# Joint stage of an encoder layer: stores on other queues, seven pairs begun, and the second sequence's key, value and query ahead of the first's merge

## The chip, the cores and the metric

One core of a Trainium2 chip. The metric is the device time of the whole kernel in microseconds, the median of several executions.

## What is computed

One layer of an encoder in fp32, for two independent sequences of 512 tokens and width 1024 ("prompt" is sequence 0, "sample" is sequence 1). Cut to what matters here:

```python
x = x + 0.5 * swiglu(rms_norm(x, ffn1_norm), ...)            # first FFN, D_FF = 2816
h = rms_norm(x, mix_norm)
aq, ak, av, mq, mk, mv, gate_pre, o_pre, g_att, g_mlstm = split(h @ w_in)
aq = apply_rope(rms_norm(aq per head, q_norm), cos, sin)     # 8 heads of 64
ak = apply_rope(rms_norm(ak per head, k_norm), cos, sin)     # 2 key/value heads
att = gqa_block_attention(aq, ak, av)                        # softmax over all 512 keys
mem = mlstm_bidirectional(mq, mk, mv, gate_pre, ..., o_pre)  # 4 heads of 128, forward and backward
merged = sigmoid(g_att) * (att @ w_up_att) + sigmoid(g_mlstm) * (mem @ w_up_mlstm)
x = x + merged @ w_out
x = x + 0.5 * swiglu(rms_norm(x, ffn2_norm), ...)            # second FFN
return rms_norm(x, final_norm)
```

## The kernel before, in words

**Tiles.** A sequence lies transposed, as 8 tiles of 128 channels x 512 tokens. An fp32 product is made of fp32r products of high and low halves (`hi`, `lo`), three for each pair of tiles; a weight is split into its halves by one operation of ScalarE and one of VectorE, from a raw tile (four buffers, `wr`) into a split tile (four buffers, `w8`). Weights that the second sequence needs again are stored split to DRAM (`wpark`, L236) and loaded from there (L228). Work tiles of 128x512 come from a ring of eleven (`T2`) and one of four (`F2`). PSUM has the banks `mm` (3), `pss` (2), `pst` (2) and `pso` (1).

**Stages.** The first FFN for both sequences (to about 660 us); then mixing (to about 1477 us); then the second FFN. Mixing is written as a generator `mix(s, ...)` for each sequence, `m0` and `m1`, which the main program resumes by `next` so that stages of the two alternate.

**The end of the first FFN.** The down products give each output tile in turn, first of sequence 0, then of sequence 1; `done1` stores each and adds up squares. At the last tile of sequence 0 it makes the statistics and all eight normed tiles in one go (`normed`, store to `xnbuf`, `put`); the statistics of sequence 1 come behind the key/value product of mix (`early`).

**Mixing of sequence 0.** `tok_proj` for key/value/gates, then for query (L724). The raw query and key rows go to DRAM (`qkbuf`). Then the joint stage, `Joint`: eleven pairs of output columns (4 of mLSTM query and key, 2 of output gates, 4 of memory gates, 1 of attention gates) are computed for both sequences together with a Strassen-like scheme of seven block products for each pair. `begin` makes the first two of them (24 products of 128x512), which need only the left normed blocks of sequence 0; `right_sums` makes the sums of blocks (`xc`, L253, L257 to L260) that the other five need (60 products); `whole` makes those, and all 84 for a pair not begun. Five pairs are begun (`BEGUN`). The results (`emit`) go to DRAM: `joint_q`, `joint_k` as halves (L1429, L1430), the others through a tanh (L1433, L1436). Behind each `whole` stands one of eleven *pieces* of sequence 0: gates, key piece, four query pieces, four maxima pieces, scales. A query piece loads a raw row, sums squares (L778, L779), takes the reciprocal root on GpSimd (L165, L167, tile `rs`), applies rope on VectorE, splits, transposes on PE in two groups of four (L956) into the one bank `pso`, copies (L957) and stores (`qtbuf`, L958). The pieces share four rows.

**Behind it.** Attention of sequence 0 loads `kv` and `qT` from these buffers; then four memory heads (scores L1163, transposes L1205, products L1213, statistics L177 and L187, with the units of `merge_att` between), then `merge_mem` (L740, tiles `pss` and `pst`), which needs the memory heads' output `mem`. Then `m1` runs its own key/value and query products, keeping rows in SBUF, and `q_rope` and `k_turn` lie beside eight output units of sequence 0 (`out_unit`). Attention, memory heads, merge and output units of sequence 1 follow.

**What sets the order.** The code's order and small shifts of priority (`shifted`) are turned into one instruction list for each engine before the run; an engine takes its list in order. SyncE (SP) issues nearly all transfers before the change, and its queue is in order as well: a store that waits for its data holds up the loads behind it.

## Time and profile before

| | us |
|---|---|
| median of 3 runs (lowest, highest) | 2130.81 (2128.25, 2133.09) |
| the profiled execution: time | 2128.62 |
| the profiled execution: span in the trace | 2126.7 |
| PE busy | 2053.2 |
| mean granted clock of PE | 0.988 |

The span runs from the first instruction to the last. A row of the timeline gives start, duration, engine, line, operation, tiles, shape and count; in brackets the idle time before it and what ended that. A row of waits gives the line that waited, what released it, then total us, times and longest. `L307` is the line of the Strassen-like products in both FFNs and in the joint stage, so its rows are told apart by their time.

### The profile page before, as it was taken

The page shows a single profiled execution, that of the slowest core. Times are in us where ns is not written, and L with a number is a line of the kernel's source. Part 1 is how long each engine was busy: PE and PEld are TensorE (multiplying, and loading weights), DVE is VectorE, ACT ScalarE, POOL GpSimd, SP SyncE. Part 2 cuts the span into 40 slices and gives each one's busy share as a digit, 9 for nine tenths or more (in the row PEclk, how much of TensorE's full clock was granted, in tenths as well). Part 3 has the DMA queues.
Part 4 walks back from the last instruction along what each step waited for, and adds up shares of the span by engine and source line. Part 5 has one row for each costly group of instructions (what it writes and reads, how often), then busy time and mean ns, then how long its engine had stood idle before and what let it go on. Part 6 is the DMA issues. An engine that isn't in the chain of part 4 may idle for free.

```text
span 2126.7 us, 27181 instructions
## 1 busy us (share of the span) xinstructions
PE 2053.2 (97%) x9356; PEld 1675.9 (79%) x9356; DVE 1547.5 (73%) x2611; ACT 973.5 (46%) x1801; POOL 140.2 (7%) x156
## 2 busy tenths in 40 slices
PE   8999999999998899899998999989999999999998
PEld 6888888888887677687877877778888888888887
DVE  6887776767785686649686778674878777786696
ACT  7544444532224444346674446542644444443222
POOL 1000000001013002200012110001000000000000
PEclk9999999999999999999999999999999999999999
DMA  9655654799756955556567862667755564499753
GB/s 285 196 191 165 225 177 158 240 340 335 260 194 251 285 173 159 148 188 234 208 208 260 279 214 86 217 200 258 247 168 193 177 219 169 159 342 349 271 199 114
DMA packets 322506, 464.82 MB, mean 219 GB/s; under 512 B 21600, under 2 KB 180336, under 8 KB 320960
## 3 DMA queue, kind: packets, MB, share of 16 engines
q1 hardware_dynamic: 321776, 461.82, 64.3%
q0 software_dynamic: 592, 1.27, 0.3%
q8 instruction: 74, 1.21, 0.2%
q14 instruction: 64, 0.52, 0.1%
HBM read 295.07 MB, written 167.94 MB: 218 GB/s over the span
## 4 chain that ended last, share of the span: by engine, by line
PE 86%; DVE 5%; DMA 4%; ACT 2%; issue 1%; POOL 1%; SPq 0%; DVEq 0%; POOLq 0%; ACTq 0%
PE pss L307 20%; PE pst L307 13%; PE mm L307 11%; PE mm L574 8%; PE mm L740 8%; PE pss L574 4%; PE pst L574 4%; PE mm L724 4%; PE pso L574 3%; PE pso L1069 1%; PE pss L1042 1%; PE pst L1061 1%; PE pso L724 1%; PE pst L740 1%; PE pso L1213 1%
## 5 line engine op out<-in xcount | busy, mean ns | idle before, releaser
L307 PE MATMUL pss<-xc,w 128*128 128x512 f32 x1320 | 325.3, 395 | 8.3 <-ACT w L265 6.7
L307 PE MATMUL pst<-xc,w 128*128 128x512 f32 x1320 | 324.0, 390 | 2.3 <-ACT xc L252 2.3
L307 PE MATMUL mm<-xc,w 128*128 128x512 f32 x1320 | 315.4, 391 | 4.5 <-ACT f L315 1.7
L307 PEld LDWEIGHTS pss<-xc,w 128*128 128x128 f32 x1320 | 248.3, 190 | 65.2 <-ACT w L265 7.1
L307 PEld LDWEIGHTS mm<-xc,w 128*128 128x128 f32 x1320 | 247.1, 188 | 59.4 <-ACT f L315 3.9
L307 PEld LDWEIGHTS pst<-xc,w 128*128 128x128 f32 x1320 | 247.7, 188 | 54.3 <-ACT xc L252 3.0
L265 ACT ACTIVATE w<-t 128x512 fp32r<-128x512 f32 x220 | 134.4, 628 | 204.9 <-DVE t L291 56.3
L266 DVE TENSOR_TENSOR w<-t,w 128x512 fp32r<-128x512 f32 x220 | 149.8, 696 | 84.6 <-ACT w L265 81.0
L574 PE MATMUL mm<-rt,w 128*128 128x512 f32 (+1 forms) x819 | 191.0, 387 | 3.8 <-DVE xs L591 3.8
L574 PEld LDWEIGHTS mm<-rt,w 128*128 128x128 f32 x819 | 152.6, 189 | 34.2 <-DVE xs L591 4.2
L307 PE MATMUL pss<-xc,f 128*128 128x512 f32 x660 | 162.2, 395 | 6.3 <-DVE t L1479 6.2
L307 PEld LDWEIGHTS pss<-xc,f 128*128 128x128 f32 x660 | 125.4, 191 | 34.4 <-DVE t L1479 8.0
L642 ACT ACTIVATE w<-t 128x512 fp32r<-128x512 f32 x82 | 51.6, 632 | 111.5 <-PE pst L574 68.3
L642 ACT ACTIVATE w<-wr 128x512 fp32r<-128x512 f32 x72 | 44.6, 630 | 125.7 <-PE pso L574 68.6
L266 DVE TENSOR_TENSOR w<-wr,w 128x1024 fp32r<-128x1024 f32 x55 | 67.3, 1223 | 38.8 <-ACT w L265 38.7
L574 PE MATMUL pss<-rt,w 128*128 128x512 f32 x396 | 93.7, 389 | 0.0
L574 PE MATMUL pst<-rt,w 128*128 128x512 f32 x396 | 93.7, 389 | 0.0
L574 PEld LDWEIGHTS pss<-rt,w 128*128 128x128 f32 x396 | 74.3, 188 | 15.4
L574 PEld LDWEIGHTS pst<-rt,w 128*128 128x128 f32 x396 | 74.3, 188 | 15.4
L265 ACT ACTIVATE w<-wr 128x1024 fp32r<-128x1024 f32 x55 | 58.2, 1058 | 51.6 <-PE pst L307 17.9
L740 PE MATMUL mm<-mh,w 128*128 128x512 f32 x256 | 79.9, 391 | 0.0
L643 DVE TENSOR_TENSOR t<-pst,t 128x512 fp32r<-128x512 f32 x96 | 65.0, 687 | 19.7 <-ACT t L642 18.5
(405 smaller groups left out, 3549.7 us busy)
## 6 DMA issues: line engine op xcount, KB each, us to landing
rt<-rbuf SPq DMA_DIRECT2D x154, 512.0 KB, 5.7
wr<-in_ffn_w_gate_dram SPq DMA_DIRECT2D x62, 512.0 KB, 5.3
wpark<-w SPq DMA_DIRECT2D x60, 512.0 KB, 4.1
w<-wpark SPq DMA_DIRECT2D x60, 512.0 KB, 5.4
rbuf<-tab SPq DMA_DIRECT2D x102, 256.0 KB, 3.9
wr<-in_ffn_w_up_dram SPq DMA_DIRECT2D x44, 512.0 KB, 4.2
wr<-in_w_in_dram SPq DMA_DIRECT2D x40, 512.0 KB, 4.9
rbuf<-f SPq DMA_DIRECT2D x72, 256.0 KB, 4.1
```

The costliest lines, as they stand in the source:

```text
L265: pin(nc.scalar.activation(t[:, 0], src, AF.Copy))
L266: pin(V_.tensor_tensor(t[:, 1], src, f(t[:, 0]), op=ALU.subtract))
L307: nc.tensor.matmul(p, a[:, k, :], xt[:, b, k, :], start=(first and k == 0 and i == 0), stop=(k == HK_ - 1 and i == 2), skip_group_check=True)
L574: nc.tensor.matmul(p, u[:, a, d * P:(d + 1) * P], r[:, b, ts], start=(first and q == 0 and k == 0), stop=(q == len(us) - 1 and k == 2), sk ...
L642: nc.scalar.activation(hi, src, AF.Copy)
L643: (eng or V_).tensor_tensor(lo, src, f(hi), op=ALU.subtract)
L724: nc.tensor.matmul(p[b][:, :N], src(k)[a][:, bs], w_[:, kl, :], start=(k == 0 and i == 0), stop=(k == KD - 1 and i == 2))
L740: nc.tensor.matmul(p, a[:, k, :], b, start=(k == 0 and i == 0), stop=(k == n - 1 and i == 2))
L1042: nc.tensor.matmul(p, qT[:, h, b * P:(b + 1) * P], kv[:, hk * 2 + j, :], start=(j == 0), stop=(j == 1))
L1061: nc.tensor.transpose(p[:, b * P:(b + 1) * P], Ps[b][:, kb * P:(kb + 1) * P], ident)
L1069: nc.tensor.matmul(po, Vst[:, kv_, hk, :], w, start=(kv_ == 0 and i == 0), stop=(kv_ == 3 and i == 1))
L1213: nc.tensor.matmul(po, vm[:, a, t, hs_], b, start=(t == 0 and n == 0), stop=(t == 3 and n == 2))
```

## The change

1. **End of the first FFN.** `done1` makes the normed tiles of sequence 0 one by one, each with a tile of sequence 1 (in the order of d + 4), and the statistics of sequence 1 at its fourth tile; `early` is gone. The `xnbuf` store goes to GpSimd's queue.
2. **Stores.** `wpark` and the low halves of joint q and k, the output gates and the value rows go to GpSimd's queue; high halves, memory and attention gates, `kept`, `qkbuf`, `qtbuf` and the key rows go to ScalarE's. The loads of a piece (`qkbuf`, `ebuf`) go to GpSimd's queue. `kvbuf`, `qtbuf` and `qkbuf` exist once for each sequence.
3. **Seven pairs begun** in place of five, in the order (1, 2), (3, 4), (5), (6) behind the four steps of right sums.
4. **Sequence 1 goes the way of sequence 0**: its key/value and query rows go to DRAM, and its eleven pieces replace `k_turn` and `q_rope`. Its two products stand behind the last memory head of sequence 0 and ahead of that sequence's `merge_mem`; the pieces stand one behind each `merge_mem` unit, with rows of the common ring and the bank `pso`. Five of sequence 0's output units follow at once, three go into the queue of sequence 1's attention.
5. **Dealing.** The six attention gates that a sequence computes itself go to DRAM and come back at `merge_att`; the `merge_att` units are dealt evenly over the memory heads, in the order 6, 7, 0 to 5; `merge_mem` alternates between `pss` and `mm`; the maxima of sequence 1 leave its attention for its pieces.

The diff, cut to its core:

```diff
-            nc.sync.dma_start(d[:, i], f(t))
+            nc.gpsimd.dma_start(d[:, i], f(t))          # wpark
...
         def q_piece(b, rows, bank):
             t, o, m, out = rows
-            nc.sync.dma_start(t, qkbuf[:, b, :])
+            nc.gpsimd.dma_start(t, qkbuf[s][:, b, :])
...
                 nc.scalar.activation(out, p, AF.Copy)
-                nc.sync.dma_start(qtbuf[:, g * 4:g * 4 + 4, b * P:(b + 1) * P], out.rearrange("p (h t) -> p h t", t=P))
+                nc.scalar.dma_start(qtbuf[s][:, g * 4:g * 4 + 4, b * P:(b + 1) * P], out.rearrange("p (h t) -> p h t", t=P))
...
+        queue.extend(merge_att(d) for d in (6, 7, 0, 1, 2, 3, 4, 5))
         for h in range(HM):
...
-            queue.append(merge_att(2 * h))
-            fill(1)
+            fill(-(-len(queue) // (8 - 2 * h)))
             mem_out(h, Ts)
-            queue.append(merge_att(2 * h + 1))
-            fill(99)
-
+            fill(-(-len(queue) // (7 - 2 * h)))
+            if h in (1, 2) and not s:
+                for d in range(4):
+                    prep1(4 * (h - 1) + d)
+        flush()
+
+        pieces = yield
         mh, ml = A([P, KD, S], F32R, "mh"), A([P, KD, S], F32R, "ml")
         for d in range(KD):
             mem_gate(d)
             go(merge_mem(d))
+            if pieces:
+                pieces.pop(0)([T2() for _ in range(4)], PO)
         flush()
-        yield None
-
+        for q in pieces:
+            q([T2() for _ in range(4)], PO)
...
     def done1(s, d, _):
         nc.sync.dma_start(xbuf[s][:, d, :], xs[s][:, d, :])
-        accs[s] = sq_add(xs[s][:, d, :], accs[s], "R", eng=V_ if s == 0 and d == KD - 1 else None)
-        if s == 0 and d == KD - 1:
-            mid_stats(0)
-            for i in (B11, B21):
-                xm[i] = xc_tile()
-            for k in range(KD):
+        last = d == (KD - 1, HK_ - 1)[s]
+        accs[s] = sq_add(xs[s][:, d, :], accs[s], "R", eng=V_ if last else None)
+        if last:
+            mid_stats(s)
+        if s:
+            k = (d + HK_) % KD
+            if k % HK_ == 0:
+                xm[(B11, B21)[k // HK_]] = xc_tile()
+            with shifted(20):
                 xt = xs[0][:, k, :]
                 normed(xt, gm, R[0], k)
-                nc.sync.dma_start(xnbuf[:, k, :], xt)
+                nc.gpsimd.dma_start(xnbuf[:, k, :], xt)
                 put(xm[B11 if k < HK_ else B21], k % HK_, xt)
...
-                nc.sync.dma_start(to[:, 0, :], hi)
-                nc.sync.dma_start(to[:, 1, :], lo)
+                nc.scalar.dma_start(to[:, 0, :], hi)
+                nc.gpsimd.dma_start(to[:, 1, :], lo)
...
-    BEGUN = 5
+    BEGUN = 7
...
-        if k + 1 < BEGUN:
-            jn.begin(k + 1, jn.left(k + 1))
+        for j in ((1, 2), (3, 4), (5,), (6,))[k]:
+            jn.begin(j, jn.left(j))
...
-    next(m0)
-    m1 = mix(1, lambda k: [t[:, k, :] for t in nhl[1]], None, lambda: stats2(0), prep2)
-    next(m1)
-    next(m0)
-    next(m1)
-    acc2[0] = next(m0)
-    next(m1)
-    next(m1)
-    acc2[1] = next(m1)
+    m0.send([])
+    m1 = mix(1, lambda k: [t[:, k, :] for t in nhl[1]], lambda: stats2(0), prep2)
+    pieces = next(m1)
+    units, acc = m0.send(pieces)
+    go(*units[:5])
+    flush()
+    acc2[0] = acc
+    m1.send(units[5:])
+    units, acc = m1.send([])
+    go(*units)
+    flush()
```

The order of the instructions at three places. First SP, at the start of the joint stage, where the rows of the right sums are first loaded (from `xbuf` and `xnbuf`; `wr` are raw weights of pairs). Before:

```order
L206 DMA wr_5743<-in_w_in_dram 128x8x128
L1445 DMA kept_0_289<-f_395_5522 128x512
L206 DMA wr_5799<-in_w_in_dram 128x8x128
L1429 DMA joint_q_5524<-t_390_5517 128x512
L1541 DMA t_389_5516<-xbuf_111 128x512
L1430 DMA joint_q_5524<-t_391_5518 128x512
L1541 DMA t_387_5514<-xnbuf 128x512
```

and now:

```order
L206 DMA wr_5642<-in_w_in_dram 128x8x128
L206 DMA wr_5678<-in_w_in_dram 128x8x128
L206 DMA wr_5734<-in_w_in_dram 128x8x128
L206 DMA wr_5770<-in_w_in_dram 128x8x128
L206 DMA wr_5825<-in_w_in_dram 128x8x128
L1480 DMA t_385_5571<-xbuf_111 128x512
L1480 DMA t_383_5569<-xnbuf 128x512
```

The stores have left SP, and two more raw weights, those of the two further pairs, stand ahead of the first row.

Second PE, behind the products of the last memory head of sequence 0 (its statistics are L177 and L187 in both). Before, `merge_mem` of sequence 0 (operand `mem`) follows:

```order
L1213 MATMUL pso_8999<-t_968_9039,Vm_8451 128x512
L177 MATMUL pst_9051<-ident,t_969_9048 128x128 x4
L187 MATMUL pst_9061<-ident,rs_9058 128x128
L740 MATMUL pst_9144<-mem_8209,w_9089 128x512 x9
L187 MATMUL pst_9061<-ident,rs_9058 128x128 x3
```

and now products of key and value of sequence 1 (`xh`, `xl` are its normed tiles as halves):

```order
L1147 MATMUL pso_9076<-t_944_9116,Vm_8482 128x512
L724 MATMUL mm_9191<-w_9188,xh_8762 128x272
L724 MATMUL mm_9191<-w_9188,xl_8763 128x272
L724 MATMUL mm_9191<-w_9188,xh_8762 128x272 x2
L724 MATMUL mm_9191<-w_9188,xl_8763 128x272
L724 MATMUL mm_9191<-w_9219,xh_8762 128x272
L177 MATMUL pst_9128<-ident,t_945_9125 128x128 x4
```

The products of 128x272 now stand around the statistics; `merge_mem` has gone behind all of them and the query's.

Third GpSimd (POOL) beside `merge_mem` of sequence 0, where the pieces of sequence 1 now stand: it issues the stores of split weights (L236), loads the key row (L889) and the first query row (L912), makes low halves of the merged rows (L643) and the reciprocal roots:

```order
L236 DMA wpark_9694<-w_9691 128x1024 x2
L236 DMA wpark_9808<-w_9805 128x1024
L889 DMA t_1001_9519<-qkbuf_5201 128x512
L236 DMA wpark_9808<-w_9805 128x1024
L236 DMA wpark_9936<-w_9933 128x1024
L643 TENSOR_TENSOR ml_9441<-mg_8233,mh_9440 128x512
L236 DMA wpark_9936<-w_9933 128x1024
L165 TENSOR_SCALAR rs_9527<-ssk_9524 128x8
L167 TENSOR_TENSOR rs_9527<-rs_9527,nhalf 128x8
L643 TENSOR_TENSOR ml_9441<-mg_8233,mh_9440 128x512
L912 DMA t_1016_9600<-qkbuf_5201 128x512
```

Before, this stretch of POOL's list held the six L643 operations and nothing else ahead of sequence 1's gates; now a load of a row can be issued only when the stores listed ahead of it have their split weights.

177 lines of the change are left out of this document (57 added, 120 removed).

## The prediction

> **What bounds the kernel now.** I read the page first: who is busy, and who stands in the chain that ended last.
>
> ```profile
> PE 2053.2 (97%) x9356; PEld 1675.9 (79%) x9356; DVE 1547.5 (73%) x2611; ACT 973.5 (46%) x1801; POOL 140.2 (7%) x156
> PE 86%; DVE 5%; DMA 4%; ACT 2%; issue 1%; POOL 1%; SPq 0%; DVEq 0%; POOLq 0%; ACTq 0%
> ```
>
> TensorE (PE) is the bound: it works 2053.2 of 2126.7 us. The change leaves the products as they are, so it can win only PE's 73.5 us of idle time and what a slow clock costs behind a gap. The view of waits, for PE, says what ended the gaps (total, times, longest):
>
> ```profile
> PE pst L187 <- POOL rs L167: 11.3, 8, 2.4
> PE pss L307 <- ACT w L265: 6.7, 1, 6.7
> PE pso L956 <- issue: 6.6, 3, 3.2
> PE pst L1205 <- DVE t L1191: 6.2, 4, 2.5
> PE pss L307 <- DVE t L1479: 6.2, 3, 3.6
> ```
>
> Nearly all of these lines belong to the joint stage and the stretches beside it. The table by windows places them (first PE's busy us of each 50, then PEld, DVE, ACT, POOL, the granted clock, DMA share, GB/s):
>
> ```profile
> 650.00:700.00 50.00, 43.99 (x232) 37.50 (x231) 23.48 (x37) 20.71 (x39) 11.97 (x18) 0.97 0.84 290
> 700.00:750.00 50.00, 39.35 (x162) 30.35 (x161) 39.52 (x60) 26.66 (x44) 0.96 (x1) 0.86 0.80 249
> ...
> 800.00:850.00 50.00, 45.51 (x198) 36.97 (x197) 31.64 (x51) 21.75 (x40) 10.72 (x11) 0.93 0.52 158
> 850.00:900.00 50.00, 42.02 (x178) 33.55 (x177) 31.17 (x47) 20.07 (x36) 14.35 (x10) 0.93 0.47 133
> ...
> 1100.00:1150.00 50.00, 42.37 (x189) 32.89 (x190) 36.34 (x74) 24.44 (x51) 8.52 (x8) 0.93 0.73 233
> ```
>
> I count a window's loss as its idle time plus 50 us times what the clock lacks: 6.0 + 1.5 = **7.5** at 650, 10.7 + 7.0 = **17.7** at 700, 4.5 + 3.5 and 8.0 + 3.5 = **19.5** from 800 to 900, 7.6 + 3.5 = **11.1** at 1100. The clock term is no invention of the view: in PE's timeline the same twelve products take longer behind a gap (start, duration, idle before).
>
> ```profile
> 843.99 2.88 PE L307 MATMUL pst<-xc,w 128*128 128x512 f32 x12
> ```
>
> ```profile
> 871.38 4.28 PE L307 MATMUL pss<-xc,f 128*128 128x512 f32 x12 [2.23 <-DVE t L1479]
> ```
>
> 2.88 us without a gap (2.72 from start to start, 0.227 a product), 4.28 behind 2.23 us of idling: a gap costs itself and about 1.4 us more.
>
> **A, the end of the first FFN (650 to 700).** PE stands 3.76 us ahead of the last down product:
>
> ```profile
> 657.87 3.87 PE L574 MATMUL mm<-rt,w 128*128 128x512 f32 x9 [3.76 <-DVE xs L591]
> ```
>
> and those nine products take 3.87 us instead of nine times 0.227, 2.0. The change spreads the eight normed rows of the first sequence over the second's rows and moves the second's statistics ahead, so that VectorE has less in one heap. I take 4 of the 7.5 us; the ends are 0 (the heap is only spread over the same stretch) and 7. Eight xnbuf stores and eleven weight stores go to POOL there, among its additions of squares. A POOL issue costs more than one on SP (0.93 against 0.42 us):
>
> ```profile
> 476.97 0.93 POOL L672 DMA_DIRECT2D f<-in_c_rope_dram  x1
> ```
>
> ```profile
> 708.88 0.32 SPq L1429 DMA_DIRECT2D joint_q<-t  x1
> 709.25 0.42 SPq L1541 DMA_DIRECT2D t<-xbuf  x1
> ```
>
> **B, the start of the joint products (700 to 750).** The largest single gap is here:
>
> ```profile
> 741.59 1.22 PE L307 MATMUL pss<-xc,w 128*128 128x512 f32 x2 [6.67 <-ACT w L265]
> ```
>
> The first whole pair needs all right sums, and VectorE is full from the first loaded row on (60 instructions, 39.5 us in this window, and the front of it waited for loads). Two more pairs begun are 2 x 24 products x 0.227 = 10.9 us of PE work that needs no right sum, set ahead of that wait; each adds to VectorE two splits and a correction, about 1.2 us. So the gap of 6.7, one of 2.3 behind it and part of the slow clock should go: at most 10.9 - 2.4 = 8.5. The loads of the rows also lose their stores: on SP the first L1541 stood behind joint_q's, which waited for its split. But the order of SP shows two more weight loads ahead of the first row now, and with four buffers for raw weights these wait for earlier splits; that gives back 1 to 3 us. I take **8** (ends 3 and 14).
>
> **C, the pieces of the first sequence (800 to 900).** Each q piece is one long chain with four rows and one bank. One turn in the timelines of PE, ScalarE, SP and POOL:
>
> ```profile
> 832.81 1.09 PE L956 MATMUL pso<-ident,f 128*128 128x128 f32 x4 [3.21 <-issue]
> ```
>
> ```profile
> 833.93 0.60 ACT L957 ACTIVATE R<-pso 128x512 f32<-128x512 f32 x1 [0.90 <-PE pso L956]
> ```
>
> ```profile
> 839.64 0.59 ACT L957 ACTIVATE R<-pso 128x512 f32<-128x512 f32 x1
> ```
>
> ```profile
> 834.55 6.07 SPq L958 DMA_DIRECT2D qtbuf<-R  x2
> ```
>
> ```profile
> 845.29 1.67 POOL L167 TENSOR_TENSOR rs<-rs,nhalf 128x8 f32<-128x8 f32 x1
> ```
>
> ```profile
> 853.76 0.63 PE L956 MATMUL pso<-ident,f 128*128 128x128 f32 x4 [2.14 <-issue]
> ```
>
> The turn is 20.95 us. Between the turns PE has one whole pair, 60 products or 13.6 us, and eight transposes. The two copies stand 5.7 us apart because the second needs the first's store landed, and those stores share SP with loads and joint stores. The view of transfers (count, KB each, median us from issue to landing) gives the price of a store, of a piece's load, and of loads that POOL issued elsewhere:
>
> ```profile
> qtbuf<-R SPq DMA_DIRECT2D x8, 256.0 KB, 2.3
> ```
>
> ```profile
> f<-qkbuf SPq DMA_DIRECT2D x5, 256.0 KB, 3.6
> ```
>
> ```profile
> t<-in_final_norm_dram POOLq DMA_DIRECT2D x2, 256.0 KB, 4.6
> tab<-in_c_tri_dram POOLq DMA_DIRECT2D x1, 256.0 KB, 6.6
> ```
>
> On ScalarE's own queue the copies can stand 0.6 + 2.3 + 0.3 = 3.2 us apart: 2.5 us less, and near 1 less behind the second store, so 4 pieces x 3 = 12 of chain at best. Against it, the load of each piece now comes from POOL (4.6 to 6.6 us, against 3.6 from SP): 1 to 3 us where the load ends the wait. I take **5** (ends -8, if four loads each end the wait 2 to 3 us later and the stores give little, and 14).
>
> The Trainium skill, in "DMA: Bandwidth & Descriptors", section "Rules for kernel authors", says that spreading transfers over SP, ACT and GpSimd brings no bandwidth and saves only the issuing sequencer's time. By that rule C would bring eight issues of 0.32 us, 2.6. The trace bears it out as far as the DMA share goes (0.47 to 0.52 here, so that bandwidth is not what is short), but the 6.07 us of SP for two stores is waiting in line, not moving bytes.
>
> **D, the tail of the last memory head of the first sequence (1100 to 1150).** Today merge_mem stands right behind it and needs its output, so PE runs dry:
>
> ```profile
> 1120.17 1.41 PE L1205 MATMUL pst<-ident,t 128*128 128x128 f32 x8 [1.09 <-DVE t L1191]
> ```
>
> ```profile
> 1131.19 0.32 PE L187 MATMUL pst<-ident,rs 128*128 128x128 f32 x1 [2.22 <-POOL rs L167]
> ```
>
> In the new order the second sequence's key/value/query products, which need nothing of that head, lie between. Their length is in PE's timeline today, from key/value's first product to the first output unit behind query's last:
>
> ```profile
> 1151.85 0.41 PE L724 MATMUL mm<-w,xh 128*128 128x272 f32 x2
> ...
> 1186.62 0.62 PE L740 MATMUL mm<-mh,w 128*128 128x512 f32 x2
> ```
>
> That is 34.8 us, against a tail of some 17 us (1120 to 1137). It is hidden whole, except its own transposes: **9** of 11.1 (ends 6 and 11).
>
> **E, what is new: the second sequence's pieces behind merge_mem.** This is the place that can spoil the change. Before, the second sequence's q and k stayed in SBUF, and eight output units (8 x 24 products x 0.227 = 43.6 us) covered rope and transposes. The windows from there into the second attention:
>
> ```profile
> 1200.00:1250.00 50.00, 48.15 (x240) 38.59 (x239) 39.29 (x77) 19.26 (x40) 7.27 (x6) 1.00 0.83 276
> 1250.00:1300.00 50.00, 49.02 (x248) 38.37 (x247) 46.35 (x108) 28.52 (x66) 1.27 (x2) 1.00 0.33 111
> 1300.00:1350.00 50.00, 49.78 (x246) 39.17 (x245) 36.33 (x82) 29.59 (x68) 0.00 (x0) 1.00 0.53 184
> ```
>
> It cost 1.9 us. Now ten pieces run through DRAM while PE has merge_mem (96 products, 21.8 us) and, in the order of PE, the 72 products of three output units (16.3 us) and 48 transposes (about 4 us): 42 us from merge_mem's start to the first scores. The chain beside it: key piece, then four q pieces on VectorE. I count 47 rows of VectorE from key's sum of squares to the last split, at 0.66 us (39.5 us by 60 in the window at 700) 31 us; four waits for POOL's rs at 1.7 to 2.4 us, 8 us; ahead of it the key load from POOL, which stands behind seven weight stores, 5 us, and square and sum, 1.4 us; behind it transposes, copy, store (3.2 us) and the load of qT:
>
> ```profile
> qT<-qtbuf SPq DMA_DIRECT2D x2, 1024.0 KB, 6.8
> ```
>
> The sum is 31 + 8 + 6 + 10 + 1 = 56 us; some of the head may lie in the query products, since key is there before them. So PE should stand 56 - 42 = 14 us; I take 3 off for the head and add 2 for the clock, and the 1.9 us goes: **-11** net (ends +1, if the head and POOL's waits are all hidden, and -30, if each of nine pieces waits 2 us more for its four rows: there are eleven such buffers, and the gates' loads take theirs out of them).
>
> **The rest.** The last head of the second sequence keeps its tail. Attention of the second sequence loses its maxima (16 sums of VectorE) but PE idles only 1.0 and 0.2 us in those two windows: 0. POOL issues about 125 transfers at 0.6 to 0.9 us ahead of the rs that end 11.3 us of PE's waits: I take -2 (ends 0 and -8).
>
> **Sum.** 4 + 8 + 5 + 9 - 11 - 2 = 13 us gained. The profiled execution took 2128.6 us (span 2126.7 and 1.9 around it), 2.2 below the median of the runs, 2130.8; from the median I get 2118, from the profiled one 2116. I say **2117**.
>
> **Rivals.**
> - *The second sequence's pieces become the bound* (25%): slower. With four rows a piece and eleven buffers, at most two pieces are in flight. If each of five turns costs the 20.95 us of today's turn in half overlap, say 15, the chain from key's arrival on is 75 + 10 = 85 us against 42 + 22 of PE work (96 query products x 0.227): 21 lost in idling and 5 in clock, less the 1.9; and B and C give 6 instead of 13: 4 + 6 + 9 - 24 - 2 = -7, about **2138**. It decides from a turn of some 14 us on, where the chain is 80 us, 16 beyond the work, and eats the 17 of the rest. For it: today's turn. Against it: today's turn contains SP's queueing and a PE that takes its transposes in fixed places.
> - *POOL's queue is too slow* (7%): slower. If POOL's transfers land 3 us later than SP's did and the begun pairs' low halves hold their buffers, B gives 0 and C -8: 4 + 0 - 8 + 9 - 11 - 2 = -8, **2139**. For it the 6.6 us row; against it POOL's 7% of busy time. The Trainium skill, in "SBUF — State Buffer", section "SBUF: two separate sides", has a rule to that end: while VectorE runs an operation in a 2-port mode, GpSimd cannot write the descriptors of the transfers that it issues, and they look blocked. No row of this trace issues from POOL beside a full VectorE, so the trace neither bears it out nor denies it.
> - *Everything is covered* (13%): the pieces of the second sequence hide under merge_mem and the units, the stores give their 12: 6 + 11 + 12 + 10 - 1 - 1 = 37, **2094**.
> - *Losses and gains meet* (10%): E costs 24, all else as forecast: **2130**. That is no difference: about 0.2%, 4 us, is what a measurement of this kernel can tell.
> - *My forecast* (45%): 2106 to 2125.
>
> Faster are the forecast and full cover: 58%. Same 10%, slower 32%. The range holds 8 in 10 if it reaches from full cover to just beyond the first rival: 2094 to 2141.
>
> **What would show it.** Right: no wait of 6 us on L265's counterpart at the first whole pair; q transposes of the first sequence about 17 to 18 us apart; no idle time between the last head and merge_mem of the first sequence; one group of gaps, 10 to 16 us in all, ahead of the second sequence's first scores, ended by the load of qT or by the q transposes. Wrong: gaps in the joint stage ended by transfers from POOL, gaps at the memory heads ended by rs that grew, or a stall ahead of the second attention over 25 us.

## The result and the profile after

| | before | after |
|---|---|---|
| median of 4 runs each (lowest, highest), us | 2131.95 (2128.25, 2135.01) | 2181.86 (2179.35, 2183.35) |
| profiled execution: time; span, us | 2128.62; 2126.7 | 2182.96; 2181.2 |
| mean granted clock of PE | 0.988 | 0.981 |

The change makes the kernel slower: the ratio is 1.0234, with a 95% interval of 1.0213 to 1.0254, some 50 us. I had forecast a gain of 13. The head of the page and the chain of waits of the kernel after:

```profile
PE 2069.8 (95%) x9356; PEld 1684.8 (77%) x9356; DVE 1558.4 (71%) x2612; ACT 974.7 (45%) x1803; POOL 205.9 (9%) x285
PE 74%; DMA 10%; DVE 7%; issue 5%; ACT 2%; POOL 2%; SPq 0%; POOLq 0%; DVEq 0%; ACTq 0%
```

The products are the same 9356, yet they keep PE busy 16.6 us longer (a mean granted clock of 0.981 in place of 0.988, which is some 15 us of the span), and PE idles 111.4 us in place of 73.5. The chain leaves PE more often: transfers hold 10% of it, where they held 4%. The waits of PE:

```profile
PE pso L921 <- issue: 9.1, 4, 2.8
PE pst L307 <- DVE w L266: 8.2, 1, 8.2
PE pss L307 <- ACT t L1408: 6.7, 4, 2.9
PE pss L307 <- DVE t L1418: 6.0, 1, 6.0
PE pst L187 <- POOL rs L167: 5.5, 6, 1.3
PE pso L921 <- ACT t L922: 5.3, 4, 3.3
PE mm L740 <- POOL ml L643: 4.8, 3, 2.7
PE pss L986 <- ACT t L991: 4.8, 1, 4.8
```

No single wait is large. The wait of 6.7 us at the first whole pair has become one of 8.2 on the other half of such a split (L266), the waits for rs (L187) fell from 11.3 to 5.5, and the q transposes (L921, before L956), the scores (L986) and merge_mem's halves (L643) are new or longer. The table by windows says where:

```profile
650.00:700.00 50.00, 45.82 (x240) 39.69 (x239) 33.46 (x44) 25.13 (x44) 26.20 (x44) 0.97 0.87 308
700.00:750.00 50.00, 45.95 (x204) 37.69 (x203) 34.91 (x53) 25.65 (x44) 5.93 (x8) 1.00 0.84 262
750.00:800.00 50.00, 39.83 (x172) 31.82 (x171) 35.94 (x61) 18.85 (x33) 3.79 (x7) 0.90 0.52 164
800.00:850.00 50.00, 42.54 (x184) 32.50 (x183) 32.59 (x61) 23.52 (x42) 13.09 (x18) 0.97 0.62 197
850.00:900.00 50.00, 39.75 (x171) 31.67 (x172) 26.37 (x45) 21.50 (x39) 11.80 (x15) 0.95 0.35 104
...
1100.00:1150.00 50.00, 44.65 (x255) 36.76 (x254) 35.93 (x88) 28.82 (x71) 8.30 (x10) 1.00 0.62 199
1150.00:1200.00 50.00, 47.56 (x220) 38.56 (x219) 24.52 (x43) 20.80 (x37) 19.51 (x35) 0.97 0.92 323
1200.00:1250.00 50.00, 30.98 (x106) 21.27 (x105) 35.89 (x58) 15.21 (x28) 15.63 (x20) 0.69 0.77 236
1250.00:1300.00 50.00, 44.12 (x198) 34.20 (x196) 39.34 (x80) 20.79 (x43) 12.03 (x14) 0.93 0.69 244
```

Counted as before (idle time plus 50 us times what the clock lacks): at 700 the loss went from 17.7 to 4.1, but at 750 there are 15.2 now. At 1100 it fell from 11.1 to 5.4. At 1200, where 1.9 us were lost, there are **34.5**: 19.0 of idling and 15.5 of clock (counted over all 50 us), with DVE at 35.9 us of 50.

Windows shift when a kernel grows, so I divide the loss by landmarks instead: the start of the first joint product, of the first scores, of sequence 0's first output unit and of the second FFN. The rows of PE's timeline, before:

```profile
701.31 4.13 PE L307 MATMUL mm<-xc,w 128*128 128x512 f32 x17
958.35 0.62 PE L1042 MATMUL pss<-kv,qT 128*128 128x512 f32 x2
1186.17 0.39 PE L740 MATMUL mm<-mh,w 128*128 128x512 f32 x1
1476.79 2.43 PE L307 MATMUL mm<-xc,w 128*128 128x512 f32 x10
```

and after:

```profile
703.64 1.52 PE L307 MATMUL mm<-xc,w 128*128 128x512 f32 x6
973.36 0.61 PE L986 MATMUL pss<-kv,qT 128*128 128x512 f32 x2
1204.38 0.50 PE L740 MATMUL mm<-mh,w 128*128 128x512 f32 x1 [0.54 <-DVE t L1078]
1528.71 1.52 PE L307 MATMUL mm<-xc,w 128*128 128x512 f32 x6
```

Up to the joint stage 2.3 us were lost. The trace of after was 4.3 us behind already at the first down product of the first FFN (450.43 in place of 446.13), and that start lies between 445.9 and 450.4 in the twenty traces, whatever the kernel; from it to the joint stage the kernel after gains 2.0 us. The joint stage takes 269.7 in place of 257.0, **+12.7**; from there to the output units 231.0 in place of 227.8, **+3.2**; and from there to the second FFN 324.3 in place of 290.6, **+33.7**. The second FFN adds 2.6. Two places need a cause, then: the joint stage, and the stretch in which the second sequence's pieces run. Its gaps in PE's timeline:

```profile
1194.06 0.44 PE L905 MATMUL pso<-ident,t 128*128 128x128 f32 x2 [2.44 <-ACT t L898]
...
1209.76 1.12 PE L905 MATMUL pso<-ident,t 128*128 128x128 f32 x4 [3.29 <-ACT t L907]
...
1221.21 0.79 PE L740 MATMUL mm<-ml,w 128*128 128x512 f32 x1 [2.73 <-POOL ml L643]
...
1228.37 1.11 PE L921 MATMUL pso<-ident,t 128*128 128x128 f32 x4 [3.27 <-ACT t L922]
...
1242.38 0.90 PE L740 MATMUL mm<-mh,w 128*128 128x512 f32 x2 [1.97 <-ACT mh L642]
...
1276.27 1.22 PE L986 MATMUL pss<-kv,qT 128*128 128x512 f32 x2 [4.81 <-ACT t L991]
```

It is not one wait for qT, as I had expected, but a gap every few us, at the pieces' transposes and at the output units' own operands (mh, ml) in turn.

### The profile page after: what moved, and what is told of

It is laid out like the page before. It is cut to its first block, busy times and chain, and to the rows that moved or that the text cites. A ratio compares the mean times of both kernels' runs of the same rounds, so it can differ in the third digit from the quotient of the medians.

```text
span 2181.2 us, 27389 instructions
## 1 busy us (share of the span) xinstructions
PE 2069.8 (95%) x9356; PEld 1684.8 (77%) x9356; DVE 1558.4 (71%) x2612; ACT 974.7 (45%) x1803; POOL 205.9 (9%) x285
## 4 chain that ended last, share of the span: by engine, by line
PE 74%; DMA 10%; DVE 7%; issue 5%; ACT 2%; POOL 2%; SPq 0%; POOLq 0%; DVEq 0%; ACTq 0%
PE pss L307 17%; PE pst L307 11%; PE mm L307 10%; PE mm L574 8%; PE mm L740 6%; PE pst L574 4%; PE pss L574 4%; PE mm L724 4%; PE pso L574 3%; PE pss L986 1%; PE pso L1013 1%; PE pso L724 1%; PE pst L1005 1%; PE pso L1147 1%; DMA wr<-in_ffn_w_gate_dram 1%
## 5 line engine op out<-in xcount | busy, mean ns | idle before, releaser
L266 DVE TENSOR_TENSOR w<-t,w 128x512 fp32r<-128x512 f32 x220 | 149.2, 693 | 75.9 <-ACT w L265 72.4
L307 PEld LDWEIGHTS pss<-xc,f 128*128 128x128 f32 x660 | 125.7, 192 | 34.4 <-DVE t L1418 6.9
L642 ACT ACTIVATE w<-wr 128x512 fp32r<-128x512 f32 x72 | 44.6, 630 | 128.0 <-PE pso L574 74.9
L266 DVE TENSOR_TENSOR w<-wr,w 128x1024 fp32r<-128x1024 f32 x55 | 67.2, 1223 | 44.3 <-ACT w L265 44.2
L740 PE MATMUL mm<-mh,w 128*128 128x512 f32 x256 | 86.4, 413 | 5.8 <-ACT mh L642 2.7
L642 ACT ACTIVATE t<-pst 128x512 fp32r<-128x512 f32 x96 | 55.3, 596 | 56.1 <-PE pst L1139 23.7
```

Source lines behind the costliest of these rows:

```text
L266: pin(V_.tensor_tensor(t[:, 1], src, f(t[:, 0]), op=ALU.subtract))
L307: nc.tensor.matmul(p, a[:, k, :], xt[:, b, k, :], start=(first and k == 0 and i == 0), stop=(k == HK_ - 1 and i == 2), skip_group_check=True)
L642: nc.scalar.activation(hi, src, AF.Copy)
L740: nc.tensor.matmul(p, a[:, k, :], b, start=(k == 0 and i == 0), stop=(k == n - 1 and i == 2))
```

## The experiments

Each is the kernel before or after with one thing changed; `a_` stands for after, `b_` for before. Times are medians, beside that of the kernel before on the same chip. Expectations use letters for theories: S says that the chain of copy and store in one row sets the pieces' pace, V that the pieces' own work on VectorE and GpSimd does, R that rows of the ring run short, O that the order of begun pairs spoils the joint stage, G that what begun pairs save is given back beside the pieces.

**Parts of the change apart.** All of part 2's transfers back on SP (`a_sp`), five begun pairs again (`a_begun5`), and the kernel before with part 2 alone (`b_queues`) or with seven begun pairs alone (`b_begun7`).

```diff
# a_sp, against after: every line of part 2, such as
-                nc.scalar.dma_start(qtbuf[s][:, g * 4:g * 4 + 4, b * P:(b + 1) * P], ...)
+                nc.sync.dma_start(qtbuf[s][:, g * 4:g * 4 + 4, b * P:(b + 1) * P], ...)
# a_begun5, against after
-    BEGUN = 7
+    BEGUN = 5
-        for j in ((1, 2), (3, 4), (5,), (6,))[k]:
+        for j in ((1,), (2,), (3,), (4,))[k]:
```

> The changed kernel with every transfer of part 2 of the change back on SP's queue; all else as changed. Theory Q (the queues cost the time: transfers that GpSimd issues, and stores that ScalarE issues, land later than SP's did, 3.4 to 7.1 us against 2.2 to 4.1, and hold rows and banks): the 50 us that the change lost come back for the most part, 2140 to 2155. Theory O (the new order costs it: too little work of PE beside the second sequence's pieces, and seven begun pairs that hold the rows which the right sums load into): the queues matter little, 2170 to 2195.

> The changed kernel with five pairs begun, one behind each step of right sums, as before; all else as changed. Theory O: the row loads no longer wait for the stores of two more begun pairs; PE's loss from 700 to 950 us falls from 54 us towards the 41 of the kernel before, and the time to about 2169. Theory Q: the loads wait for stores that land late, of five pairs as of seven; 2178 to 2186.

> The kernel before with part 2 of the change alone (stores and piece loads on ScalarE's and GpSimd's queues). Theory Q: slower by 15 us or more, 2146 and up, with the loss between 700 and 950 us. Theory O: within 6 us of before, 2126 to 2138.

> The kernel before with seven pairs begun in the order of the change, stores still on SP. Theory O: the two pairs hold rows of the ring, loads come later and nothing is won; 2130 to 2145. Theory Q: with stores that land in 2.3 us the two pairs cover the gap of 6.7 us as forecast: 2120 to 2126.

Measured: `a_sp` 2168.89 beside 2130.12, 1.0196 [1.0155, 1.0236]; `a_begun5` 2183.20, 1.0263 [1.0224, 1.0302]; `b_queues` 2140.31, 1.0060 [1.0035, 1.0085]; `b_begun7` 2131.59, 1.0013 [0.9996, 1.0029]. The queues cost 11 us out of the change (50 less the 39 left in `a_sp`) and 10 by themselves, so they are about a fifth of the loss (`a_sp` stands on two runs, and its interval leaves 33 to 50 us without them); by the landmarks the joint stage takes 258.0 in `a_sp`, 267.8 in `b_queues`: nearly all of its +12.7 is theirs. The seven begun pairs are worth nothing that can be measured, put in or taken out, and the part of theory O that blames the begun pairs is refuted: with five, the joint stage takes 272.1. Some 39 us are left, with all transfers on SP, and they are the second sequence's stretch, which is the other part of O (`a_sp` came 1 us short of O's band, and `b_queues` between the bands of O and Q).

**Which queue.** The kernel before with GpSimd's transfers alone (`b_poolq`: wpark, xnbuf, low halves, output gates, value rows, the pieces' loads) and with ScalarE's stores alone (`b_actq`).

```diff
# b_poolq, against before, for instance
-                nc.sync.dma_start(to[:, 1, :], lo)
+                nc.gpsimd.dma_start(to[:, 1, :], lo)
# b_actq, against before, for instance
-                nc.sync.dma_start(to[:, 0, :], hi)
+                nc.scalar.dma_start(to[:, 0, :], hi)
```

> The kernel before with only those transfers of part 2 moved that go to GpSimd's queue. If GpSimd's issues and landings are what costs the 10 us of b_queues: 2138 to 2144. If ScalarE's stores do: 2128 to 2133.

> The kernel before with only those stores of part 2 moved that go to ScalarE's queue. If GpSimd's transfers are what costs the 10 us of b_queues, this one keeps the gain that was forecast for the q pieces: 2122 to 2128. If ScalarE's stores cost, 2134 to 2142.

Measured: `b_poolq` 2145.79 beside 2130.54, 1.0070 [1.0047, 1.0093]; `b_actq` 2135.78, 1.0026 [1.0012, 1.0039]. So 15 and 5 us, together more than both at once (10), though the three intervals just leave room for a plain sum. The waits of PE in `b_poolq` show where GpSimd's 15 lie:

```profile
PE pss L307 <- DVE t L1479: 11.0, 2, 9.4
PE pst L307 <- ACT xc L252: 10.9, 1, 10.9
```

One gap of 10.9 us at the first right sums, where before had 2.3 us on that line, and one of 9.4 further on. The transfers land later there: in the view of transfers wpark's stores take 6.5 us at the median (4.1 before), the low halves 4.0 (2.4), and SP's loads of the next rows wait for joint_q's stores to land and free their buffers, 12.2 us in five waits where five took 4.3 before:

```profile
SPq L1541 <- DMA joint_q<-t: 12.2, 5, 3.4
```

That this wait makes the gap is read from the trace and was not tried apart. Even the `qtbuf` stores, still on SP, take 4.4 in place of 2.3.

**The chain of copy and store (S).** A second row for the copies of a query piece and the last key copy, so that the second copy need not wait for the first's store: in `a_sp` (`a_sp_out2`) and in before (`b_out2`).

```diff
-                nc.scalar.activation(out, p, AF.Copy)
+                to = (out, o)[g]
+                nc.scalar.activation(to, p, AF.Copy)
```

> The changed kernel with all transfers on SP (as in a_sp), and in both sequences' query pieces the second copy goes to the row o, which is dead by then, so that it does not wait for the first one's store; in the key piece the last of four copies likewise. Theory S (the stretch behind merge_mem is a chain of twelve copies, each behind the store of the one before, some 4 us apart): eight of twelve copies lose that wait; the loss of PE from 1150 to 1350 us falls from 54 by 15 or more, and the joint stage of the first sequence gains a few us too; 2145 to 2155. Theory V (the stretch is set by VectorE's and GpSimd's work on the pieces and by the eleven rows): 2163 to 2172.

> The kernel before with the same second row for copies as in a_sp_out2 and nothing else. If the store's wait is what sets the first sequence's query pieces apart (20 us a turn against 15 us of PE work), 800 to 900 us loses 6 to 12 us less: 2119 to 2125. If the rest of the chain (load, square, root, rope) sets it: 2128 to 2132.

Measured: 2174.05 beside 2129.88, 1.0210 [1.0189, 1.0230], and 2131.12, 1.0012 [0.9999, 1.0026]. Nothing is gained by it in either kernel; S falls, and with it the term C of the prediction, whose mechanism this was. The turns of the first sequence's query pieces do get shorter (from one piece's first transposes to the next's: 13.9, 14.1 and 16.9 us in `a_sp_out2`, 21.1, 20.2 and 16.1 in `a_sp`), but the joint stage takes 257.0 us in place of 258.0. So the turns are not what holds it.

**Cover, and the pieces' own work.** Eight output units issued ahead of the second attention in place of five (`a_sp_units8`), and the second sequence's pieces without sums of squares, root and rope (`a_sp_norope`), both against `a_sp`.

```diff
# a_sp_units8
-    go(*units[:5])
+    go(*units)
-    m1.send(units[5:])
+    m1.send([])
# a_sp_norope, key and query piece alike
-            ssq = small(8, "ssk")
-            sumsq(t, ssq, out)
-            qo = rope_apply(t, rstd_cols(ssq, 8), tabs[0], b, (t, o, m))...
+            if not s:
+                ssq = small(8, "ssk")
+                sumsq(t, ssq, out)
+                rope_apply(t, rstd_cols(ssq, 8), tabs[0], b, (t, o, m))
```

> As a_sp, with all eight output units of the first sequence ahead of the second's attention instead of five. Theory cover (too little PE work beside the pieces, wherever their chain spends its time): 3 x 24 products, 16 us, more cover; the loss from 1150 to 1350 falls by 8 to 14, 2155 to 2161, less what the second attention then lacks in filling. Theory place (PE's list has the pieces' transposes ahead of the units, so more units behind them cover nothing): within 5 of 2169.

> As a_sp, but the second sequence's key and query pieces leave out sums of squares, reciprocal root and rope: the raw rows are split, transposed and stored. Theory V: the chain loses 8 us of GpSimd's roots and some 25 us of VectorE; 2145 or less. Theory S: the stores keep their pace of some 4 us for each of twelve copies; 2158 to 2170.

Measured: `a_sp_units8` 2170.28 beside 2129.88, 1.0192 [1.0172, 1.0213], no change against `a_sp`. The trace says why this decides little: of the units' 192 products PE's order puts only 42 ahead of the second attention's scores (120 in `a_sp`, 72 in after), since the list that the schedule makes moved the rest behind. `a_sp_norope`: 2154.29, 1.0117 [1.0096, 1.0139], 14 us less than `a_sp`, between the bands of V and S: V has a part, over a third of the 39, and 24 us remain with all of that work gone.

**The place of the pieces.** The timeline of VectorE in `a_sp` had a pattern: merge_mem's additions (L1078, one for each of its units) do not come as fast as their products but one to a piece, ten us apart:

```profile
1205.85 0.68 DVE L1078 SCALAR_TENSOR_TENSOR t<-t,pss 128x512 f32<-128x512 f32 x1
...
1215.92 0.68 DVE L1078 SCALAR_TENSOR_TENSOR t<-t,mm 128x512 f32<-128x512 f32 x1
...
1226.74 0.69 DVE L1078 SCALAR_TENSOR_TENSOR t<-t,pss 128x512 f32<-128x512 f32 x1 [0.62 <-issue]
...
1235.19 0.69 DVE L1078 SCALAR_TENSOR_TENSOR t<-t,mm 128x512 f32<-128x512 f32 x1 [1.04 <-DMA t<-joint_mem]
```

Each output unit needs the halves of all eight units of merge_mem, and the last came at 1235. On PE the output units run as far as the halves go, and stop for the last:

```profile
1235.93 0.79 PE L740 MATMUL mm<-mh,w 128*128 128x512 f32 x1 [3.25 <-DVE t L1078]
```

So the output units, which I had counted as cover beside the pieces, waited for the pieces themselves, through the in-order list of VectorE. `a_sp_mfirst8` takes the pieces out of merge_mem (all ten behind it, eight units ahead of the attention). `a_sp_gatef2` asks the rival R: the memory gates' rows come from the ring of four, and leave the eleven to the pieces.

```diff
# a_sp_mfirst8, against a_sp, with the two lines of a_sp_units8
             go(merge_mem(d))
-            if pieces:
-                pieces.pop(0)([T2() for _ in range(4)], PO)
# a_sp_gatef2, against a_sp
-            ths[d] = T2()
+            ths[d] = T2() if s else F2()
```

> As a_sp_units8 (all transfers on SP, eight output units ahead of the second attention), but the eight merge_mem units of the first sequence stand ahead of all ten pieces of the second in the code, instead of one piece behind each. Theory M (merge goes at the pace of the pieces: each merge_mem's sums on VectorE, its half ml and its gate's row stand behind a piece, some 10 us apart, so that mh and ml are whole only some 75 us after merge_mem starts, and the output units that should cover the pieces wait for them): merge is done after some 25 us, the eight units cover, the loss from 1150 to 1350 falls from 56 us to 20 to 30; 2135 to 2147. Theory V (the pieces' own work on VectorE and GpSimd sets the length wherever they stand): 2160 or more.

> As a_sp, but the rows into which the first sequence's memory gates are loaded come from the ring of four and not from the eleven which the pieces use. Theory R (the rows set merge's pace: a gate's load waits for the row of the piece before the last): loss from 1150 to 1350 falls by 10 or more, 2150 to 2160. Theory M without rows (the order on VectorE sets it): 2164 to 2172.

Measured: `a_sp_mfirst8` 2164.23 beside 2130.54, 1.0152 [1.0129, 1.0176]; `a_sp_gatef2` 2163.63, 1.0155 [1.0122, 1.0188]. Each median is 5 us better than that of `a_sp`, but their intervals overlap, so neither gain is shown. R put `a_sp_gatef2` at 2160 or less, so the rows are a small part at most (merge_mem takes 31.0 us there, 34.4 in `a_sp`). In `a_sp_mfirst8`, merge_mem runs clean (23.0 us from its first product to the first output unit, of which 96 products x 0.227 = 21.8 are work), but PE stops later for what the pieces leave late:

```profile
1256.19 2.07 PE L986 MATMUL pss<-kv,qT 128*128 128x512 f32 x4 [7.77 <-DMA qT<-qtbuf]
...
1277.94 0.80 PE L740 MATMUL mm<-xh,w 128*128 128x512 f32 x1 [19.68 <-DVE f L1194]
```

The 19.68 us are for a row that a load brings, and in SP's queue that load stands behind the loads of the maxima pieces. So the maxima were next: `c1` puts gates and key piece ahead of merge_mem, the query pieces behind it, and the maxima and scales as units among the second attention's; `c2` is `a_sp_mfirst8` with the maxima at heads 4 to 7 of the second attention and the scales behind; `c3` is `c2` with gates and key piece ahead of merge_mem.

```diff
# c2, against a_sp_mfirst8
+            if s and h >= 4:
+                max_piece(h - 4, [T2() for _ in range(4)])
...
+        if s:
+            mem_scales()
...
-        for q in pieces:
+        for q in pieces[0:6]:
# c1, against a_sp_mfirst8 (c3 has its loops over pieces[:2] and pieces[2:6], and c2's additions)
+        for q in pieces[:2]:
+            q([T2() for _ in range(4)], PO)
...
-        for q in pieces:
+        for q in pieces[2:6]:
...
-    m1.send([])
+    m1.send([(lambda: None, lambda _, q=q: q([T2() for _ in range(4)], PO)) for q in pieces[6:]])
```

> As a_sp (all transfers on SP), but the second sequence's gates and key piece stand ahead of the first's merge_mem, the four query pieces behind all of it, all eight output units behind those, and the maxima and scales pieces go one by one into the second attention's queue. Theory P (the loss behind merge_mem is a matter of place: merge held to the pieces' pace, then output units held by the maxima's loads on SP, 19.7 us in a_sp_mfirst8): loss from 1150 to 1350 falls from 54 to 15 to 25 us, 2130 to 2142. Theory V (the second sequence's way through DRAM costs its time in any place): 2155 or more.

> As a_sp_mfirst8 (all transfers on SP; merge_mem whole, then gates, key and query pieces, then eight output units), but the four maxima pieces stand in the second attention behind heads 4 to 7 and the scales behind it, as in the kernel before, so that no maxima row is loaded ahead of the output units' rows on SP. Theory P (place): the 19.7 us ahead of the attention gates go, with some 5 us of slow clock; 2136 to 2145, and the loss from 1150 to 1350 is 18 to 28 us. Theory V (the way through DRAM costs its time in any place): 2158 or more.

> As c2, with the second sequence's gates and key piece ahead of merge_mem. Theory P: the query pieces start some 10 us earlier against the output units, the wait of 7.8 us for qT goes, and merge_mem waits up to 5 us for what stands ahead of it; 2130 to 2142. Theory V: 2158 or more.

Measured: `c1` 2182.66 beside 2129.64, 1.0246 [1.0218, 1.0275], a miss: the attention, whose queue holds maxima where it held output units, takes 269.8 us from its scores to the second FFN, 238.2 before, with as many of the units' products in it. `c2` 2156.81 beside 2128.67, 1.0137 [1.0116, 1.0157]; `c3` 2161.93, 1.0162 [1.0137, 1.0187]. So the place is worth some 11 us (39 to 28): the four runs of `c2` lie from 2155.6 to 2159.5, the six of `a_sp`, `a_sp_units8` and `a_sp_out2` from 2165.7 to 2174.5. That is far less than theory P said. `c2` falls between the bands of P and V, `c1` and `c3` fall into V's, as `a_sp_mfirst8` had done, and in `c3` the wait for qT that was to go is 7.53 us. V (the way through DRAM costs its time in any place) is therefore not excluded for the rest. What stops PE in `c2` ahead of the second attention:

```profile
1237.67 1.09 PE L921 MATMUL pso<-ident,t 128*128 128x128 f32 x4 [4.68 <-issue]
...
1253.73 2.04 PE L986 MATMUL pss<-kv,qT 128*128 128x512 f32 x4 [6.25 <-DMA qT<-qtbuf]
```

These are the waits that the prediction named for E, but it gave them behind 42 us of cover that would have been at work.

To divide what is left, the excess over before in three stretches, all from the starts of rows in PE's timeline: merge_mem (to the first output unit, less 21.8 of work), from there to the second attention's first scores (52.4 before), and from there to the second FFN (238.2 before). Where output units moved from the second stretch to the third, their products are booked back at 0.227 us.

| us | merge_mem | ahead of the scores | behind | sum |
|---|---|---|---|---|
| after (120 products booked back) | 9.4 | 24.9 | 8.8 | 43 |
| `a_sp` (72) | 12.6 | 22.7 | 2.9 | 38 |
| `a_sp_norope` (150) | 6.5 | 17.0 | 2.9 | 26 |
| `a_sp_mfirst8` (0) | 1.2 | 13.5 | 17.8 | 33 |
| `c2` (0) | 1.2 | 17.1 | 11.3 | 30 |

**Where seven begun pairs lose their gain.** `b_begun7` has 2.6 us of loss at 700 where before has 17.7, and the same time. If the gain is given back because whole pairs of begun columns (60 products) are a shorter cover for a piece than pairs not begun (84), an order with the long pairs beside the pieces should keep it (G): tried with seven begun (`b_order7`) and with five (`b_order5`).

```diff
# b_order7: against before, BEGUN = 7 as in after, and
-            order = list(range(len(pairs)))
+            order = [0, 1, 7, 8, 9, 10, 2, 3, 4, 5, 6]
# b_order5: BEGUN = 5, and
+            order = [0, 1, 5, 6, 7, 8, 2, 3, 4, 9, 10]
```

> The kernel before with seven pairs begun, and the four pairs not begun put third to sixth, where the query pieces are, so that each has 84 products beside it and not 60. Theory G (what seven begun pairs win at the start is given back where query pieces with turns of some 20 us lie beside wholes of 13.6 us): the 10 us won from 700 to 750 stay, 2118 to 2125. Else (the joint stage is held by something all through): 2128 to 2135.

> The kernel before with five pairs begun as before, and four of the pairs not begun put third to sixth, beside the query pieces. Theory G: the loss of 19.5 us from 800 to 900 falls by 8 or more, and less comes back behind it, where only maxima pieces lie beside wholes of 60 products; 2118 to 2125. Else: 2128 to 2135.

Measured: `b_order7` 2130.24 beside 2129.64, 1.0011 [0.9996, 1.0026], though its joint stage is 3.4 us shorter (253.6); `b_order5` 2132.58, 1.0007 [0.9989, 1.0025]. G is not borne out in the time, and where the gain goes stays open.

**The dealing of the merge_att units.** They alone, dealt over the memory heads of the kernel before so that some are left for the last head's tail. The prediction had no term for this part of the change.

```diff
# b_deal, against before
+        queue.extend(merge_att(d) for d in range(KD))
         for h in range(HM):
...
-            queue.append(merge_att(2 * h))
             fill(1)
             mem_out(h, Ts)
-            queue.append(merge_att(2 * h + 1))
-            fill(99)
+            fill((0, 1, 0, 99)[h])
```

> The kernel before with its merge_att units dealt 1, 2, 1 and 4 over the memory heads (three of the four behind the last head's output) instead of 2 each. The tail of the last head (11 us lost from 1100 to 1150, some 13 around 1400 in the second sequence) gets two more units, 5.4 us of PE work, in each sequence; if the earlier heads can spare them: 2120 to 2126. If they idle as much more: 2128 to 2133.

Measured: 2127.08 beside 2131.28, 0.9982 [0.9968, 0.9995]: 4 us, the only version that beats the kernel before, and at the limit of what can be told from no change. The window at 1100 loses 8.7 in place of 11.1, that from 1350 to 1550 10.1 in place of 11.2.

## Why the prediction was wrong

- **A (+4): right in sign, half the size.** From the first down product to sequence 0's key/value product the kernel after takes 211.9 us in place of 217.5, 5.6 less, and so does every kernel with part 1 of the change. Of that, 3.7 are given back up to the joint stage (41.3 us in place of 37.6), so that some 2 stay. PE waits 2.50 us there for an addition of the down products (L591, at 665.74), which stands in VectorE's list behind a weight split and one of the normed rows that were spread.
- **B (+8): the gap moved.** The two begun pairs do fill it: 17.7 to 4.1 at 700. The first whole pair then waits for its weights, 8.21 us:

```profile
760.47 4.84 PE L307 MATMUL pst<-xc,w 128*128 128x512 f32 x11 [8.21 <-DVE w L266]
```

  VectorE's list has that split behind a row that SP loads, 6.85 us late (L638, at 757.25). I had put what is late next at one to three us; alone, in `b_begun7`, the sum is nil by the end of the stage.
- **C (+5): the wrong sign, and beyond its range's lower end (-8).** Part 2 alone makes the joint stage 10.8 us longer (`b_queues`, 267.8 in place of 257.0). I expected turns of 17 to 18 us, from one turn of 20.95; the three of the kernel before are 16.3, 21.0 and 22.8. The transposes after:

```profile
859.08 0.63 PE L921 MATMUL pso<-ident,f 128*128 128x128 f32 x4 [2.83 <-issue]
...
878.98 0.63 PE L921 MATMUL pso<-ident,f 128*128 128x128 f32 x4 [2.38 <-issue]
...
897.36 0.63 PE L921 MATMUL pso<-ident,f 128*128 128x128 f32 x4 [2.75 <-issue]
```

  are 19.9 and 18.4 us apart (the first turn is 20.3), and the same kind of gap stands before each. So the turns became neither much shorter nor longer. The copies did close up as predicted in kind, but less (4.8 us in place of 5.7 at 839, 3.2 expected), because a store from ScalarE's queue lands in 4.7 us, not 2.3:

```profile
qtbuf<-R ACTq DMA_DIRECT2D x8, 256.0 KB, 4.7
```

  I had carried a duration from SP's queue to ScalarE's. But `b_out2` and `a_sp_out2` show that the copies' distance, and the turns that it sets, are worth nothing in the time. The loads of the pieces stand on GpSimd behind its arithmetic; the output gates' scaling (L1374) waited 5.25 us for ScalarE, and a query piece's load stood behind it:

```profile
839.12 0.69 POOL L1374 TENSOR_SCALAR t<-t,hn 128x512 f32<-128x512 f32 x1 [5.25 <-ACT t L1372]
839.76 0.64 POOL L912 DMA_DIRECT2D f<-qkbuf  x1
```

  SP's queue had the same fault; the change exchanged one in-order queue for another. The stage's largest new losses lie elsewhere: 15.2 us at 750 (3.5 before), the wait under B, and 10.0 at 900 (none before), where PE waits 6.01 us for L1418, which VectorE does behind sums that wait for the maxima rows. B and C together are the joint stage's +12.7, and `a_sp` and `b_queues` show that it is the queues' price.
- **D (+9): right in mechanism, at the lower end in size (6).** The window at 1100 goes from 11.1 to 5.4, no gap lies between the last head and merge_mem, and from the first scores to the output units the kernel gains 6.2 us if merge_mem is left out (the stretch is 3.2 longer in all, but 9.4 of that are merge_mem's excess). A part of this may be the dealing's, which alone takes 2.4 out of that window (`b_deal`); the new place of the products was not tried by itself.
- **E (-11): the step that failed.** It cost some 43 us. I had set 56 us of chain against 42 of PE work "beside" it, and both sides of that sum were wrong. The cover was no cover: merge_mem's additions stand one behind each piece in VectorE's list, and each output unit needs all eight of them, so that 38 of the 42 us went at the pieces' pace (merge_mem's products take 31.2 us in place of 21.8, and the first scores start 81.3 us after the first of them). And the chain was longer. After, these are merge_mem's first product, key's load and its sum of squares, the last transposes, the load of qT and the first scores:

```profile
1173.19 2.88 PE L740 MATMUL pss<-mem,w 128*128 128x512 f32 x12
...
1177.66 0.55 POOL L889 DMA_DIRECT2D t<-qkbuf  x1
...
1184.16 0.69 DVE L773 TENSOR_REDUCE ssk<-t 128x8 f32<-128x512 f32 x1
...
1239.76 0.66 PE L921 MATMUL pso<-ident,t 128*128 128x128 f32 x4 [0.69 <-ACT t L922]
...
1243.90 0.32 SPq L975 DMA_DIRECT2D qT<-qtbuf  x1
...
1254.52 1.07 PE L986 MATMUL pss<-kv,qT 128*128 128x512 f32 x4
```

  With 6.8 us for the landing of qT that is 73 us where the sum has 56. From key's sum of squares to the last split VectorE takes 54.5 us, where the sum has 31 + 8 = 39. The pieces' own rows (some 30 us) and the waits for rs (9.3) are near what I had set; left out were 10.5 us of merge_mem's additions and weight splits that stand between them in VectorE's list, and 8 us of other waits, 6.1 of them for rows that were loaded and squared late (all these overlap by some 3 us). With merge_mem out of the pieces the same stretch takes 44.6 us (`c2`), with it 53.2 (`a_sp`). Taking the pieces out of merge_mem and the maxima out of the way (`c2`) gives back 11 us, taking the pieces' own arithmetic away 14; the two were not tried together, so they may overlap. With either, 24 to 28 us remain. Of `c2`'s, 17 lie ahead of the second attention (11 of them the two waits shown) and 11 behind its first scores, where the maxima are again as in the kernel before: PE idles there 7 us more than before and takes 4 us longer over the same products (a mean clock of 0.97 in place of 0.99), without one large wait. What causes that second part **stays open**.
- **The rest (-2).** That the second attention neither gains nor loses was wrong by 9 us (the table's third column; 3 with all transfers on SP), and that the waits for rs would grow was wrong the other way: 11.3 fell to 5.5. Dealing merge_att alone does not do that (13.1 in `b_deal`); what does was not tried apart.
- **The rivals.** "The second sequence's pieces become the bound" named the place. Its price, 24, was little over half of 43, since it kept all 42 us of work as cover, too. "POOL's queue is too slow" is true by itself (`b_poolq`, +15), and, as its trace reads, by the way given: stores that land later hold their buffers. The rule that GpSimd cannot write its transfers' descriptors while VectorE runs an operation in a 2-port mode (the Trainium skill, "SBUF — State Buffer", "SBUF: two separate sides") is not seen in the issues: 0.54 to 0.58 us each from 705 to 755, where VectorE is busy 35 of 50 us. Whether it has a part in the later landings, no run here shows. The rule weighed under C, that spreading transfers over queues saves issue time only (the Trainium skill, "DMA: Bandwidth & Descriptors", "Rules for kernel authors"), the runs agree with in so far as nothing was gained, and they go beyond it: spreading alone cost 10 us (`b_queues`), while the windows of the joint stage after show a DMA share of 0.35 to 0.84, so that bandwidth was not what ran out.

## What to carry to other kernels

Work counts as cover for a chain only if nothing in it waits for that chain; follow its operands through every engine's in-order list (here: PE's units, through VectorE's additions, to the pieces), not along PE alone. And a chain is as long as the lists that it passes through: count the other rows that stand between its own. A stage that stood behind eight units of ready work should not be moved to where its cover is produced. And a queue that is held up by waiting rather than by bandwidth is not relieved by another in-order queue whose engine has waits of its own: price the move by transfers that this queue has carried, and by the buffers that a later landing holds.

## What the runs showed of the hardware

- The same 256 KB store of the joint stage (`qtbuf`, first sequence) lands, at the median, in 2.3 us from SP before, 3.2 from ScalarE's queue alone (`b_actq`), 4.7 in the full change; and in 4.4 from SP when only GpSimd's transfers were moved (`b_poolq`). The second sequence's eight, from ScalarE's queue too, land in 2.5 in the full change, and with all on SP (`a_sp`) the first sequence's take 3.5: the issuing queue alone does not set the landing.
- The penalties of the two queues did not add up: +15 with GpSimd's, +5 with ScalarE's, +10 with both (the intervals just leave room for a sum).
- Nearly half of what the window from 1200 to 1250 lost is the clock: PE idles 19.0 us, and the mean granted clock of the window is 0.69, which counted over its 50 us is 15.5 more.
